# Putting a chunk's column sums behind its last query product, and normalising the second chunk behind all of the first

## The chip, the cores and the metric

The kernel runs on one core of one Trainium2 chip. The metric is the device time in microseconds (us) of one execution. A core has five engines with a queue of instructions each, and an engine works through its own queue in order: TensorE (PE, matrix products; PEld is its weight load), VectorE (DVE), ScalarE (ACT), GpSimd (POOL) and SyncE (SP, which only starts DMAs here). Engines wait for each other by semaphores. Matrix products write to PSUM banks, and a bank can be written again only when its result has been read out ("evacuated").

## What is computed

One layer of a hybrid decoder: a normalised input is projected into the operands of three mixers (stick-breaking attention, a Mamba-2 scan, latent attention), whose outputs are joined and projected back, and a gated feed-forward block and a last norm follow. The change lies in the very first part, the norm and the first projections:

```python
def rmsnorm(x, g):
    xf = x.astype(F32)
    y = xf * lax.rsqrt(jnp.mean(xf * xf, axis=-1, keepdims=True) + EPS)
    return (y * g.astype(F32)).astype(x.dtype)
...
        hn = rmsnorm(h, mix_norm_g[i])
        proj = hn @ w_in[i].astype(dt)
        sb_q, sb_k, sb_v, ssm_z, ssm_xbc, ssm_dt, c_q, c_kv, k_r = jnp.split(proj, split_at, axis=-1)
```

All tensors are float32; there are 1024 tokens and 16 meta tokens, 1024 features and one layer.

## The kernel before, in words

Tensors stand feature-major: 8 tiles of 128 features by 1040 tokens. Each float32 operand of a product is split into a rounded part ("hi") and the rest ("lo"), and each product is done as three: hi by hi, lo by hi, hi by lo (`dense_fm`, lines 147 to 149: 8 feature tiles by 3, so 24 products into one PSUM bank; there are two such banks, `d_ps`, used in turn).

The 1040 tokens are worked on in three chunks of 272, 384 and 384 columns (chunks 0, 1, 2). To start the products early, chunks 0 and 1 aren't normalised first. Their operands are the input times the gain alone (`first_operands`, lines 239 and 240: ACT writes the hi part `hnh`, DVE the lo part `hnl`), and the result is multiplied by the reciprocal root mean square of each token when it is evacuated. That factor comes from `chunk_rstd`: ACT squares the 8 tiles, DVE adds them up in `acc` (line 255), PE sums `acc` over the features by three small products (`ssum`, line 158), DVE scales the sums (`rc`, lines 167 and 169), POOL takes the power -0.5 (line 170), PE spreads the result over all partitions (`rrow`, line 176) and ACT copies it into `row` (line 262).

Then for chunk i the loop at line 648 issues the key product (weights `wk`), the query product (`wq`) and the value products of its token blocks (`sb_values`, lines 575 to 577, weights `wv`, banks `v_ps`). The key's evacuation `k_evac` multiplies by `row` (DVE, line 596: `scaled`) and splits into `K` and `KS` (ACT lines 603 and 604, DVE lines 605 and 606); the query's does the same into `Q` (lines 612 and 613). The lo parts of the first weights are made by POOL, one subtraction each (line 231), the hi parts by ACT (line 230).

Chunk 2, and all later products, use normalised operands: `normalise` multiplies by gain and `row` (DVE, line 270), rounds (ACT, line 271) and subtracts (DVE, line 272), 8 tiles each. `normalise(2)` is put behind the query evacuation of chunk 0 (`issue_after(scored)`), and `normalise(0)` and `normalise(1)` both behind `normalise(2)`. The first product that reads normalised chunks 0 and 1 is that of the step sizes (`step_sizes`, line 432, weights `whi`, `wlo`), which follows the value products of chunk 2 and a few score products (`sc_ps`, line 685).

A scheduler sets the order of each engine's queue at build time, by priorities that the code hands out (`high_priority`) and by `issue_after`, which keeps what is written under it behind a given instruction; PE, DVE and ACT each get one fixed order. So a change at the start can also turn neighbours round much later in the program.

Of the kernel before, what the change touches and what calls it, by code (L numbers as in the profile page):

```python
# [21 lines left out]
KT = D // 128  # L22
SEQ = 1024
META = 16
# [15 lines left out]
CH_ALL = [(0, 272), (272, 384), (656, 384)]  # L40
CH_REAL = [(0, 512), (512, 512)]
CH_SHORT = [(0, 384), (384, 384), (768, 256)]
BLOCKS = [(0, META)] + [(META + 128 * b, 128) for b in range(NQ)]
# [16 lines left out]
def tile_hybrid_block(ctx: ExitStack, tc: tile.TileContext, a: dict):  # L60
# [3 lines left out]
    PE, DVE, ACT, SP = (getattr(mybir.EngineType, e) for e in ("PE", "DVE", "Activation", "SP"))  # L64

    def last_on(engine):
        return next(i for i in reversed(nc.cur_bb.bb.instructions) if i.engine == engine)

    def f32(ap):
        return ap.bitcast(F32)  # L70
# [68 lines left out]
    def dense_fm(dpool, w, nkt, m, mov, chunks, evac):  # L139
        hi, lo = w  # L140
        for c0, n in chunks:
            ps = dpool.tile([128, 512], F32, tag="d", name="d_ps")
            for kt in range(nkt):
                mh, ml = mov(kt, c0, n)
                wh = hi[:, kt * m : (kt + 1) * m]
                wl = lo[:, kt * m : (kt + 1) * m]
                pe.matmul(ps[:m, :n], wh, mh, start=(kt == 0), stop=False)  # L147
                pe.matmul(ps[:m, :n], wl, mh, start=False, stop=False)  # L148
                pe.matmul(ps[:m, :n], wh, ml, start=False, stop=(kt == nkt - 1))  # L149
            with tc.high_priority(offset=1000):  # L150
                evac(ps, c0, n)

    def token_rstd(cols, ps, squares, blocks, width, bufs=1):


        for e, (t0, w) in enumerate(blocks):
            for i, sq in enumerate(squares):
                pe.matmul(
                    ps[:w, e : e + 1], sq[:, t0 : t0 + w], ones[:, 0:1], start=(i == 0), stop=(i == len(squares) - 1)
                )  # L160
        nb = len(blocks)
        r = cols.tile([128, nb], F32, tag=f"rc{nb}", bufs=bufs, name="rc")
        e0 = 0
        if blocks[0][1] < 128:
            w = blocks[0][1]
            dve.memset(r[:, 0:1], 1.0)
            dve.tensor_scalar(r[:w, 0:1], ps[:w, 0:1], 1.0 / width, EPS, ALU.mult, ALU.add)
            e0 = 1
        dve.tensor_scalar(r[:, e0:nb], ps[:, e0:nb], 1.0 / width, EPS, ALU.mult, ALU.add)
        pool.tensor_tensor(r, r, mhalf[:, :nb], op=ALU.pow)  # L170
        return r
# [8 lines left out]
    dpool = ctx.enter_context(tc.tile_pool(name="dpsum", bufs=2, space=PSUM))  # L180
# [15 lines left out]
    def fill_tile(tag, name):  # L196
        return fl.tile([128, 388 if tag == "craw" else 384], F32, tag=tag, name=name)
# [36 lines left out]
    def first_operands(i):  # L234

        c = slice(CH_ALL[i][0], sum(CH_ALL[i]))
        for k in range(KT):
            g = gmix[:, k : k + 1]
            act.activation(HH[k][:, c], xT[:, k, c], AF.Identity, scale=g)
            dve.scalar_tensor_tensor(HL[k][:, c], xT[:, k, c], g, f32(HH[k][:, c]), ALU.mult, ALU.subtract)  # L240

    def chunk_rstd(i):
        c0, n = CH_ALL[i]
        blocks = [(t0 - c0, w) for t0, w in BLOCKS[3 * i : 3 * i + 3]]
        if i == 2:
            squares = [raws[k // 2][:, 512 * (k % 2) :][:, :n] for k in range(KT)]
        else:
            acc = fill_tile("cacc", "acc")[:, :n]
            squares = [acc] + [sqs[k % 2][:, 512 * (k // 2 % 2) :][:, :n] for k in range(1, KT)]
        acc = squares[0]  # L250
        for k in range(KT):
            x = xT[:, k, c0 : c0 + n]
            act.activation(squares[k], x, AF.Square)
            if k > 0:
                dve.tensor_tensor(acc, acc, squares[k], op=ALU.add)
        ssum = ps0.tile([128, 4], F32, tag="ssum", name="ssum")
        with tc.high_priority(offset=200):
            r = token_rstd(p0, ssum, [acc], blocks, D, bufs=3)
            rrow = ps0.tile([128, 512], F32, tag="rrow", bufs=1, name="rrow")
            spread(rrow, r, blocks, 0)  # L260
            row = p0.tile([128, 384], F32, tag="row", bufs=3, name="row")
            act.copy(row[:, :n], rrow[:, :n])
        return r, row

    def normalise(i, row):
        c0, n = CH_ALL[i]
        c = slice(c0, c0 + n)
        for k in range(KT):
            hn = xT[:, k, c]
            dve.scalar_tensor_tensor(hn, hn, gmix[:, k : k + 1], row[:, :n], ALU.mult, ALU.mult)  # L270
            act.copy(HH[k][:, c], hn)
            dve.tensor_tensor(HL[k][:, c], hn, f32(HH[k][:, c]), op=ALU.subtract)
# [346 lines left out]
    proj, k_evac, q_evac = sb_project(0)  # L619
# [5 lines left out]
    w_k = first_weight(raws[0], a["w_sbk"][0], *first_pair("wk"), (dve, pool), dve)  # L625
    load_x(0, (2, 4, 6))
    first_operands(0)
    w_q = first_weight(raws[1], a["w_sbq"][0], *first_pair("wq"), (pool,))
    stats = [chunk_rstd(0)]
    w_v = []  # L630
    for u in range(2):
        both = value_tile("wv")
# [14 lines left out]
    sp.dma_start(acol, a["a_log"].partition_broadcast(128))  # L647
    for i, (q0, qn) in enumerate(((0, 256), (256, 384), (640, 384))):
        c0, n = CH_ALL[i]
        if i == 0:  # L650
            first_operands(1)
            stats += [chunk_rstd(1), chunk_rstd(2)]
        if i < 2:
            r, row = stats[i]
            dense_fm(dpool, w_k, KT, 128, hn_mov, [(c0, n)], lambda ps, t0, m: k_evac(ps, t0, m, row[:, :m]))
            t1 = META + q0 - c0
            dense_fm(dpool, w_q, KT, 128, hn_real, [(q0, qn)], lambda ps, t0, m: q_evac(ps, t0, m, row[:, t1 : t1 + m]))
            scored = last_on(DVE)
            sb_values(0, w_v, range(3 * i, 3 * i + 3), r, ps0)
            if i == 0:  # L660
                with tc.issue_after(scored):
                    normalise(2, stats[2][1])
                normal = last_on(DVE)
            with tc.issue_after(normal):
                normalise(i, row)
        else:
            dense_fm(dpool, w_k, KT, 128, hn_mov, [(c0, n)], k_evac)
            dense_fm(dpool, w_q, KT, 128, hn_real, [(q0, qn)], q_evac)
            sb_values(0, w_v, range(3 * i, 3 * i + 3), None, ps0)
    p0_st.close()  # L670

    with ctx_sb as st:
# [40 lines left out]
        for p in range(4):  # L713
            sb_attend(p, proj, values)
            if p < 3:
                if p == 1:
                    sb_values(1, [load_w(a["w_sbv"][1, u]) for u in range(2)], range(9))
                proj, k_evac, q_evac = sb_project(p + 1)
# [20 lines left out]
    with ExitStack() as st:  # L739
# [159 lines left out]
        for b, (t0, w) in enumerate(BLOCKS):  # L899
            ps = bank()  # L900
# [493 lines left out]
    acc = [squares(0, fs, eng) for fs, eng in (((0, 1, 2), pool), ((3, 4, 5), dve), ((6,), dve), ((7,), dve))]  # L1394
# [3 lines left out]
    with tc.high_priority(offset=400):  # L1398
        r = row_sums(acc)
        summed = last_on(PE)  # L1400
        row = row_spread(*r)
# [15 lines left out]
    acc = [squares(1, (0, 1, 4), pool)]  # L1417
# [14 lines left out]
    with tc.high_priority(offset=400):  # L1432
        r = row_sums(acc)
        summed = last_on(PE)
        row = row_spread(*r)
# [238 lines left out]
    r1, row = last_part(512, 256, between=r0)  # L1674
    last_norm(0, 512, row, (3, 6), 2)
    r2, row = last_part(768, 256, True, r1)
# [90 lines left out]
```

## Time and profile before

| | us |
|---|---|
| median of 3 runs | 1768.85 |
| the runs | 1763.76, 1768.85, 1770.01 |
| the profiled execution | 1767.26 |
| its span on the core | 1765.5 |

| engine | busy us | share of the span |
|---|---|---|
| PE | 1704.5 | 97% |
| DVE | 1143.8 | 65% |
| ACT | 846.2 | 48% |
| POOL | 721.3 | 41% |

The 1.8 us between the profiled execution and its span lie around the program and don't change with it. PE is busy nearly all of the time, so its idle stretches, and the stretches in which it runs at the lower of its two clock levels, are what an edit of the order can win or lose. In a timeline row the first number is the start, the second the length in us, and the bracket at the end is the time that the engine idled before and what ended that. Rows of one kind are merged (x8).

### The profile page before, as it was taken

Reading aid. Unit: us, or ns where it says so; the run is one execution under the profiler, and the core shown is the slowest. Engines: PE = TensorE matmul, PEld = TensorE weight load, DVE = VectorE, ACT = ScalarE, POOL = GpSimd, SP = SyncE. Lnnn points to the kernel's source line nnn. Section 1 sums busy time; section 2 is a strip of 40 time slices with the busy share of each in tenths; the row PEclk is TensorE's granted clock in tenths of the full one; section 3 lists DMA queues with packets and bytes.
Section 4 is the critical chain, followed back from the end, with each engine's and each line's share of the span. In section 5 each row is a group of like instructions: output and inputs, shape, how many; then the busy total and the mean of one; then the engine's idle time right before and its main releaser. Section 6 shows DMA issues by size and latency. Waiting matters only on the chain. (4 is left out here: it accounts for less than half of the span.)

```text
span 1765.5 us, 26574 instructions
## 1 busy us (share of the span) xinstructions
PE 1704.5 (97%) x9801; PEld 1496.5 (85%) x9801; DVE 1143.8 (65%) x1742; ACT 846.2 (48%) x1797; POOL 721.3 (41%) x498
## 2 busy tenths in 40 slices
PE   8979999999998999999999999999999999999998
PEld 7869989999987778998888878778888888878887
DVE  7678767678544673555575646986566766678644
ACT  6545565656466646676454425432322232244332
POOL 3234335334467566563331346544455545200012
PEclk9999999999999999999999999999999999999998
DMA  4222232222443546347331443122323223999602
GB/s 161 73 64 64 65 91 73 59 66 74 127 130 114 187 158 175 112 125 235 121 90 31 121 147 111 60 84 96 114 96 108 96 90 106 310 388 374 245 1 96
DMA packets 145638, 222.35 MB, mean 126 GB/s; under 512 B 24722, under 2 KB 84148, under 8 KB 145508
## 3 DMA queue, kind: packets, MB, share of 16 engines
q1 hardware_dynamic: 126112, 205.09, 36.0%
q10 hardware_dynamic: 19396, 15.56, 2.8%
q8 instruction: 77, 1.26, 0.3%
q14 instruction: 53, 0.43, 0.1%
HBM read 157.56 MB, written 63.04 MB: 125 GB/s over the span
## 5 line engine op out<-in xcount | busy, mean ns | idle before, releaser
L147 PE MATMUL d_ps<-hnh,whi 128*128 128x384 f32 (+6 forms) x744 | 249.8, 336 | 12.1 <-DVE KS L606 9.9
L149 PE MATMUL d_ps<-hnl,whi 128*128 128x384 f32 (+6 forms) x744 | 246.6, 332 | 0.0
L148 PE MATMUL d_ps<-hnh,wlo 128*128 128x384 f32 (+6 forms) x744 | 246.1, 331 | 0.0
L136 POOL TENSOR_TENSOR wlo<-wraw,whi 128x1024 fp32r<-128x1024 f32 (+1 forms) x57 | 141.1, 2475 | 227.0 <-ACT whi L134 226.2
L147 PEld LDWEIGHTS d_ps<-hnh,whi 128*128 128x128 f32 (+1 forms) x744 | 140.5, 189 | 18.0 <-issue 11.5
L149 PEld LDWEIGHTS d_ps<-hnl,whi 128*128 128x128 f32 (+1 forms) x744 | 140.8, 189 | 2.9 <-issue 0.2
L148 PEld LDWEIGHTS d_ps<-hnh,wlo 128*128 128x128 f32 (+1 forms) x744 | 140.6, 189 | 3.0 <-issue 0.5
L1274 PE MATMUL b_ps<-T,wl 128*128 128x512 f32 x352 | 138.8, 394 | 1.3 <-POOL wl L1105 1.3
L1275 PE MATMUL b_ps<-T,wh 128*128 128x512 f32 x352 | 138.2, 394 | 1.3 <-DVE T L1105 1.3
L1273 PE MATMUL b_ps<-T,wh 128*128 128x512 f32 x352 | 139.1, 396 | 0.0
L311 DVE TENSOR_TENSOR pl<-ptg,ph 128x512 fp32r<-128x512 f32 (+1 forms) x160 | 99.3, 627 | 43.0 <-ACT ph L310 41.5
L1104 ACT CAST op<-raw 128x1024 fp32r<-128x1024 f32 x69 | 71.3, 1050 | 108.1 <-PE d_ps L1559 64.4
L1105 DVE TENSOR_TENSOR op<-raw,op 128x1024 fp32r<-128x1024 f32 x69 | 84.8, 1239 | 41.6 <-ACT op L1104 41.5
L693 DVE TENSOR_TENSOR_SCAN cm<-cm,zcol 128x144 f32<-128x144 f32 (+3 forms) x64 | 101.8, 1594 | 13.3 <-ACT cm L691 12.9
L310 ACT CAST ph<-ptg 128x512 fp32r<-128x512 f32 (+1 forms) x160 | 85.2, 543 | 51.8 <-PE ptg L327 29.7
L1105 POOL TENSOR_TENSOR wlo<-raw,whi 128x1024 fp32r<-128x1024 f32 x18 | 45.4, 2523 | 109.5 <-ACT whi L1104 109.5
L1105 POOL TENSOR_TENSOR wl<-raw,wh 128x512 fp32r<-128x512 f32 x46 | 74.4, 1625 | 29.4 <-ACT wh L1104 29.4
L1104 ACT CAST wh<-raw 128x512 fp32r<-128x512 f32 x88 | 53.1, 616 | 66.4 <-PE b_ps L1275 66.3
L1111 POOL TENSOR_TENSOR tt<-tt 128x512 f32<-128x512 f32 (+1 forms) x8 | 8.1, 1012 | 186.7 <-ACT tt L1629 186.5
L134 ACT CAST whi<-wraw 128x1024 fp32r<-128x1024 f32 (+1 forms) x57 | 59.0, 1035 | 48.6 <-DMA wraw<-in_w_o_dram 17.2
L1274 PEld LDWEIGHTS b_ps<-T,wl 128*128 128x128 f32 x352 | 66.5, 189 | 16.8 <-POOL wl L1105 1.6
L1275 PEld LDWEIGHTS b_ps<-T,wh 128*128 128x128 f32 x352 | 66.3, 188 | 16.7 <-DVE T L1105 1.6
(442 smaller groups left out, 5171.9 us busy)
## 6 DMA issues: line engine op xcount, KB each, us to landing
raw<-in_w_down_dram SPq DMA_DIRECT2D x99, 256.0 KB, 5.3
s_hops<-gs SPq DMA_DIRECT2D x63, 256.0 KB, 2.0
raw<-s_hops SPq DMA_DIRECT2D x63, 256.0 KB, 5.3
raw<-in_w_gate_dram SPq DMA_DIRECT2D x22, 512.0 KB, 3.6
raw<-in_w_up_dram SPq DMA_DIRECT2D x22, 512.0 KB, 4.0
wraw<-in_w_o_dram SPq DMA_DIRECT2D x16, 512.0 KB, 4.2
wraw<-in_w_xbc_dram SPq DMA_DIRECT2D x12, 512.0 KB, 3.6
s_xs<-csig SPq DMA_DIRECT2D x24, 192.0 KB, 2.4
```

The costliest lines, as they stand in the source:

```text
L136: pool.tensor_tensor(lo[:, :cols], raw[:, :cols], f32(hi[:, :cols]), op=ALU.subtract)
L147: pe.matmul(ps[:m, :n], wh, mh, start=(kt == 0), stop=False)
L148: pe.matmul(ps[:m, :n], wl, mh, start=False, stop=False)
L149: pe.matmul(ps[:m, :n], wh, ml, start=False, stop=(kt == nkt - 1))
L310: act.copy(ph[:, :n], pt[:, :n])
L311: dve.tensor_tensor(pl[:, :n], pt[:, :n], f32(ph[:, :n]), op=ALU.subtract)
L693: dve.tensor_tensor_scan(rev, rev, zcol.to_broadcast([128, n_all]), 1.0, ALU.mult, ALU.add)
L1104: act.copy(hi, value)
L1105: eng.tensor_tensor(lo, value, f32(hi), op=ALU.subtract)
L1273: pe.matmul(banks[j], hi[:, ks], UH[u][k], start=start and k == 0, stop=False, skip_group_check=skip)
L1274: pe.matmul(banks[j], lo[:, ks], UH[u][k], start=False, stop=False, skip_group_check=skip)
L1275: pe.matmul(banks[j], hi[:, ks], UL[u][k], start=False, stop=stop and k == 3, skip_group_check=skip)
```

## The change

`chunk_rstd` is split in two. `chunk_squares` holds the squares and their sum, `chunk_rstd` the small products and what follows them. The key and query products of chunks 0 and 1 are issued with an evacuation that only remembers its arguments (`held`); for chunk 0 the small products are kept behind the last query product (`issue_after(last_on(PE))`), the operands and sums of chunks 1 and 2 follow, and then the evacuations of both products are issued, at high priority. `normal` is moved on after each `normalise`, so that chunk 1 is normalised behind all of chunk 0.

```diff
-    def chunk_rstd(i):
+    def chunk_squares(i):
         c0, n = CH_ALL[i]
...
             if k > 0:
                 dve.tensor_tensor(acc, acc, squares[k], op=ALU.add)
+        return acc
+
+    def chunk_rstd(i, acc):
+        n = CH_ALL[i][1]
+        blocks = [(t0 - CH_ALL[i][0], w) for t0, w in BLOCKS[3 * i : 3 * i + 3]]
         ssum = ps0.tile([128, 4], F32, tag="ssum", name="ssum")
...
-    stats = [chunk_rstd(0)]
+    first = chunk_squares(0)
...
-        if i == 0:
-            first_operands(1)
-            stats += [chunk_rstd(1), chunk_rstd(2)]
         if i < 2:
+            t1 = META + q0 - c0
+            held = []
+            dense_fm(dpool, w_k, KT, 128, hn_mov, [(c0, n)], lambda *at: held.append(at))
+            dense_fm(dpool, w_q, KT, 128, hn_real, [(q0, qn)], lambda *at: held.append(at))
+            if i == 0:
+                with tc.issue_after(last_on(PE)):
+                    stats = [chunk_rstd(0, first)]
+                first_operands(1)
+                stats += [chunk_rstd(e, chunk_squares(e)) for e in (1, 2)]
             r, row = stats[i]
-            dense_fm(dpool, w_k, KT, 128, hn_mov, [(c0, n)], lambda ps, t0, m: k_evac(ps, t0, m, row[:, :m]))
-            t1 = META + q0 - c0
-            dense_fm(dpool, w_q, KT, 128, hn_real, [(q0, qn)], lambda ps, t0, m: q_evac(ps, t0, m, row[:, t1 : t1 + m]))
+            with tc.high_priority(offset=1000):
+                k_evac(*held[0], row[:, :n])
+                q_evac(*held[1], row[:, t1 : t1 + qn])
...
             with tc.issue_after(normal):
                 normalise(i, row)
+            normal = last_on(DVE)
```

On PE, at the end of chunk 0's key product, the order before was (`ssum` are the small products of the column sums, `wq` the query product, `wv` the value products; lines 575 to 577 of before are 579 to 581 of the changed file):

```order
L149 MATMUL d_ps<-hnl_146,wk 128x272
L147 MATMUL d_ps<-hnh_131,wq 128x256
L158 MATMUL ssum<-ones,acc 16x1
L158 MATMUL ssum<-ones,acc 128x1 x2
L575 MATMUL v_ps<-wv,hnh_131 16x256
L576 MATMUL v_ps<-wv,hnl_139 16x256
```

In the changed kernel the same place and, 22 query products further on, the place behind the last of them read:

```order
L149 MATMUL d_ps<-hnl_146,wk 128x272
L147 MATMUL d_ps<-hnh_131,wq 128x256
L579 MATMUL v_ps<-wv,hnh_131 16x256
L580 MATMUL v_ps<-wv,hnl_139 16x256
...
L149 MATMUL d_ps<-hnl_146,wq 128x256
L158 MATMUL ssum<-ones,acc 16x1
L158 MATMUL ssum<-ones,acc 128x1 x2
L579 MATMUL v_ps<-wv,hnh_131 128x256
L580 MATMUL v_ps<-wv,hnl_139 128x256
L581 MATMUL v_ps<-wv,hnh_131 16x256
```

The small products moved behind all 24 query products and six value products. The two value products that now follow them already belong to chunk 1.

On DVE, between the evacuations of chunk 1 and the end of the normalising, the order before was (384 wide are chunks 1 and 2, 272 wide is chunk 0; the first row of line 270 is chunk 2; `K<-d_ps` and `KS<-d_ps` empty the key bank of chunk 2):

```order
L606 TENSOR_TENSOR KS<-scaled,K 64x384
L596 TENSOR_TENSOR scaled<-d_ps,row 128x384
L613 TENSOR_TENSOR Q<-scaled,Q 64x384 x2
L270 SCALAR_TENSOR_TENSOR xT<-xT,gmix,row 128x384 x8
...
L270 SCALAR_TENSOR_TENSOR xT<-xT,gmix,row 128x272 x8
L270 SCALAR_TENSOR_TENSOR xT<-xT,gmix,row 128x384 x7
...
L270 SCALAR_TENSOR_TENSOR xT<-xT,gmix,row 128x384
L605 TENSOR_TENSOR K<-d_ps,K 64x384
L606 TENSOR_TENSOR KS<-d_ps,K 64x384
L613 TENSOR_TENSOR Q<-d_ps,Q 64x384
```

In the changed kernel the same stretch reads (lines 270, 272, 596, 605, 606 and 613 are now 274, 276, 600, 609, 610 and 617):

```order
L610 TENSOR_TENSOR KS<-scaled,K 64x384
L274 SCALAR_TENSOR_TENSOR xT<-xT,gmix,row 128x384 x8
L600 TENSOR_TENSOR scaled<-d_ps,row 128x384
...
L274 SCALAR_TENSOR_TENSOR xT<-xT,gmix,row 128x272 x7
L617 TENSOR_TENSOR Q<-scaled,Q 64x384 x2
L274 SCALAR_TENSOR_TENSOR xT<-xT,gmix,row 128x272
...
L274 SCALAR_TENSOR_TENSOR xT<-xT,gmix,row 128x384 x8
L617 TENSOR_TENSOR Q<-d_ps,Q 64x384
L609 TENSOR_TENSOR K<-d_ps,K 64x384
L610 TENSOR_TENSOR KS<-d_ps,K 64x384
```

Chunk 2's normalising moved ahead of chunk 1's query evacuation, and the second half of chunk 2's key evacuation moved ahead of the eight subtractions (line 276, 384 wide) of chunk 1.

Far behind the edit, among the gates of the Mamba part and the latent attention, POOL's order before was (`gy<-gy,gs` is the gate's product, on which the evacuation of a `d_ps` bank waits; `mlo<-st,mhi` are lo parts of the latent attention's operands):

```order
L544 TENSOR_TENSOR gy<-gy,gs 128x384
L967 TENSOR_TENSOR mlo<-st,mhi 96x1040
L517 TENSOR_TENSOR grow<-grow,sq 128x384
L967 TENSOR_TENSOR mlo<-st,mhi 96x1024
L136 TENSOR_TENSOR wlo<-wraw,whi 128x1024
```

In the changed kernel the same place reads (lines 544, 967 and 517 are now 548, 978 and 521):

```order
L978 TENSOR_TENSOR mlo<-st,mhi 96x1040
L978 TENSOR_TENSOR mlo<-st,mhi 96x1024
L548 TENSOR_TENSOR gy<-gy,gs 128x384
L136 TENSOR_TENSOR wlo<-wraw,whi 128x1024
L521 TENSOR_TENSOR grow<-grow,sq 128x384
```

Both subtractions moved ahead of the gate's product; the same is so at one other place of that stage.

## Rows read from the trace of the kernel before

**Rows 1.** The list of what PE waited for in the first 130 us: engine, tile and line, what it waited for, then total us, times and the longest.

```profile
PE d_ps L147 <- DVE KS L606: 8.4, 3, 3.4
PE d_ps L147 <- DVE wk L228: 5.6, 1, 5.6
PE ssum L158 <- DVE acc L255: 2.3, 1, 2.3
```

**Rows 2.** The timeline of PE, from the first query product to the first value products of chunk 1.

```profile
12.73 0.38 PE L147 MATMUL d_ps<-hnh,wq 128*128 128x256 f32 x1
15.46 1.14 PE L158 MATMUL ssum<-ones,acc 128*16 128x1 f32 x6 [2.35 <-DVE acc L255]
16.46 0.37 PE L575 MATMUL v_ps<-wv,hnh 128*16 128x256 f32 x1
...
17.70 0.41 PE L148 MATMUL d_ps<-hnh,wq 128*128 128x256 f32 x1
...
22.18 0.41 PE L148 MATMUL d_ps<-hnh,wq 128*128 128x256 f32 x1
...
26.34 0.28 PE L575 MATMUL v_ps<-wv,hnh 128*128 128x256 f32 x1
...
27.77 0.28 PE L575 MATMUL v_ps<-wv,hnh 128*128 128x256 f32 x1
...
31.51 0.72 PE L158 MATMUL ssum<-ones,acc 128*128 128x1 f32 x6
32.10 0.37 PE L577 MATMUL v_ps<-wv,hnh 128*128 128x256 f32 x1
```

**Rows 3.** The table by stretches: from:to and length in us, then busy us (and instructions) of PE, PEld, DVE, ACT and POOL, then PE's granted clock as a share of its upper level (1.00 is 2.4 GHz, 0.50 is 1.2 GHz), the DMA share and GB/s.

```profile
13.00:14.00 1.00, 0.11 (x1) 0.00 (x0) 1.00 (x1) 1.00 (x2) 1.00 (x1) 1.00 1.07 399
...
15.00:16.00 1.00, 0.54 (x4) 0.52 (x5) 0.40 (x1) 1.00 (x4) 1.00 (x2) 0.81 1.07 393
...
21.00:22.00 1.00, 1.00 (x7) 1.00 (x7) 1.00 (x2) 0.11 (x1) 0.31 (x1) 0.50 0.22 83
...
23.00:24.00 1.00, 1.00 (x11) 0.79 (x10) 1.00 (x3) 1.00 (x3) 0.00 (x0) 1.00 0.00 0
...
69.00:72.00 3.00, 0.14 (x2) 0.00 (x0) 1.58 (x4) 2.89 (x7) 2.40 (x2) 1.00 0.13 45
...
103.00:107.00 4.00, 0.60 (x4) 0.32 (x3) 3.89 (x8) 1.57 (x4) 0.00 (x0) 1.00 0.19 58
...
108.00:109.00 1.00, 1.00 (x3) 0.73 (x3) 1.00 (x1) 0.61 (x2) 1.00 (x2) 0.50 0.00 1
```

**Rows 4.** The timelines of ACT (first row), POOL (five rows) and DVE (two rows), the weights' hi and lo parts and what lies beside them.

```profile
12.58 1.99 ACT L230 CAST wv<-raw 128x1024 fp32r<-128x1024 f32 x2
...
12.75 2.35 POOL L231 TENSOR_TENSOR wq<-raw,wq 128x1024 fp32r<-128x1024 f32 x1 [4.32 <-ACT wq L230]
15.06 2.57 POOL L231 TENSOR_TENSOR wv<-raw,wv 128x1024 fp32r<-128x1024 f32 x1
...
18.75 2.57 POOL L231 TENSOR_TENSOR wv<-raw,wv 128x1024 fp32r<-128x1024 f32 x1
32.85 1.10 POOL L170 TENSOR_TENSOR rc<-rc,mhalf 128x3 f32<-128x3 f32 x1 [11.54 <-DVE rc L169]
...
59.65 5.27 POOL L136 TENSOR_TENSOR wlo<-wraw,whi 128x768 fp32r<-128x768 f32 x1 [19.30 <-ACT whi L134]
...
12.31 3.09 DVE L255 TENSOR_TENSOR acc<-acc,sqs 128x272 f32<-128x272 f32 x2
...
18.97 3.29 DVE L240 SCALAR_TENSOR_TENSOR hnl<-xT,gmix,hnh 128x384 fp32r<-128x384 f32 x2
```

**Rows 5.** The timeline of DVE, from chunk 1's key evacuation to the release of chunk 2's key bank.

```profile
41.63 0.56 DVE L606 TENSOR_TENSOR KS<-scaled,K 64x384 fp32r<-64x384 f32 x1
...
45.31 4.33 DVE L270 SCALAR_TENSOR_TENSOR xT<-xT,gmix,row 128x384 f32<-128x384 f32 x8
49.55 3.83 DVE L272 TENSOR_TENSOR hnl<-xT,hnh 128x384 fp32r<-128x384 f32 x8
53.30 7.10 DVE L270 SCALAR_TENSOR_TENSOR xT<-xT,gmix,row 128x272 f32<-128x272 f32 x15
60.31 2.90 DVE L272 TENSOR_TENSOR hnl<-xT,hnh 128x272 fp32r<-128x272 f32 x8
63.23 0.55 DVE L605 TENSOR_TENSOR K<-d_ps,K 64x384 fp32r<-64x384 f32 x1
...
71.33 0.56 DVE L606 TENSOR_TENSOR KS<-d_ps,K 64x384 fp32r<-64x384 f32 x1
```

**Rows 6.** The timeline of PE: the start of chunk 2's products, the first score product behind its value products, and the first product of the step sizes.

```profile
50.94 0.33 PE L147 MATMUL d_ps<-hnh,wk 128*128 128x384 f32 x1
...
67.85 0.23 PE L685 MATMUL sc_ps<-K,Q 128*128 128x144 f32 x1
...
72.03 0.34 PE L147 MATMUL d_ps<-hnh,whi 128*96 128x272 f32 x1 [2.89 <-DVE KS L606]
```

**Rows 7.** The timeline of POOL at the place of the gates that the change turns round.

```profile
746.29 1.01 POOL L544 TENSOR_TENSOR gy<-gy,gs 128x384 f32<-128x384 f32 x1 [3.60 <-ACT gs L543]
749.26 2.44 POOL L967 TENSOR_TENSOR mlo<-st,mhi 96x1040 fp32r<-96x1040 f32 x1 [1.96 <-ACT mhi L966]
...
752.62 2.40 POOL L967 TENSOR_TENSOR mlo<-st,mhi 96x1024 fp32r<-96x1024 f32 x1
```

More of the change, by code (lines that the diff above doesn't have):

```diff
@@ L240, in first_operands @@
             dve.scalar_tensor_tensor(HL[k][:, c], xT[:, k, c], g, f32(HH[k][:, c]), ALU.mult, ALU.subtract)
-    def chunk_rstd(i):
+    def chunk_squares(i):
         c0, n = CH_ALL[i]
-        blocks = [(t0 - c0, w) for t0, w in BLOCKS[3 * i : 3 * i + 3]]
         if i == 2:
```

## The prediction

> **What bounds the kernel now.** I read the page's busy shares first: PE is busy 97% of the span, so time can come only from PE's idle stretches and from stretches at its lower clock level. The list of PE's waits in the first 130 us [rows 1] is to show the reader three kinds: 5.6 us at the very start for the first weight, which the change leaves alone; 2.35 us in which the column sums of chunk 0 wait for DVE's last addition; and three waits, 8.4 us together, for a key bank that DVE has not emptied. The change touches the second kind directly and the first of the three bank waits by order.
>
> PE's timeline [rows 2] shows what the 2.35 us hold up. The sums stand behind one query product that ended at 13.11 (12.73 + 0.38); they start at 15.46, and the value products and the other 23 query products, which don't need the sums, queue behind them. Then the table by stretches [rows 3]: PE's granted clock is 1.00 (2.4 GHz) at 13 to 14 and falls to 0.50 (1.2 GHz) during 15 to 16, after the idle stretch; it is still 0.50 at 21 to 22 and 1.00 at 23 to 24. So the wait also cost some 7 us at the lower level.
>
> Why does DVE end so late? Its last two additions took 3.09 us instead of some 0.9 [rows 4]: the second one finished only as POOL's subtraction for `wq` ended at 15.10.
>
> Last, DVE's timeline and the place where PE waits on it [rows 5, 6]: chunk 2's key bank is released when the second `KS` ends at 71.89, because 7 of chunk 1's normalising products stood ahead of it; PE had run out of work at about 69 and waited 2.89 us.
>
> **The wait for the sums.** Removed: 2.35 us of idle time. What is late next? The value products need the hi part of `wv`: two casts take 1.99 us from 12.58, so the first is there at about 13.6, and PE waits 0.5 us. Six value products at the upper level take 6 x 0.119 = 0.7 us (0.119 from 12 steps between 26.34 and 27.77) and end at 14.3. The next query product needs `wq`'s lo part, ready at 15.10 [rows 4]: another 0.75 us. 2.35 - 1.25 = 1.1 us are won.
>
> **The clock.** In place of one gap of 2.35 us stand two short ones with products between them. Rows show a fall after 2.35 us of idle at 13 to 15.5 and after 3.40 us at 103 to 107, and none after 2.89 us at 69 to 72 [rows 3], so the fall isn't certain even with long gaps, and I take it that two gaps under 0.8 us don't bring it. Then 29 products (6 value, 23 query) run at 0.119 instead of 0.213 us (22.18 - 17.70 over 21 steps): 29 x 0.094 = 2.7 us. The six small sums took 1.00 us from start to next start at the lower level and 0.59 at the upper [rows 2]: 0.4 us. Together 3.1 us; 0 if the clock falls all the same.
>
> **What the later sums bring.** Query products then end at 15.10 + 23 x 0.119 = 17.8, the sums at 18.4. Two value products of chunk 1 follow at once, the second of which needs DVE's first lo part of chunk 1. DVE is free at 15.40 but blocked until POOL's first `wv` subtraction ends (17.63); then the lo part takes 0.54 and is there at 18.2, in time. For the reciprocal roots DVE has 4 such operations and 2 additions ahead of `rc`: 4 x 0.54 + 2 x 0.48 = 3.1 us (a row of 8 each at that width [rows 5]), and POOL's second `wv` subtraction, 2.35 us, holds it up once: 17.63 + 3.1 + 2.35 = 23.1. POOL's power takes 1.10 [rows 4]: 24.2. PE reaches `rrow` 39 value products after the sums, 18.4 + 4.6 = 23.0, and now waits 1.2 us for it. Before, that row was ready long ahead. The sums of chunk 1 come next: DVE has 4 lo parts and 6 additions more, 23.1 + 5.1 = 28.2; PE is there at 24.2 + 0.6 + 24 x 0.119 = 27.7 and waits 0.5 us. Behind chunk 1's last addition DVE has four additions of chunk 2 (4 x 0.48) and then reads chunk 0's key bank (some 0.4): empty at about 30.5; PE, with 19 value products more, asks for it at 31. New waits: 1.7 us. If PE is at its lower clock it comes later and these waits vanish, so clock and waits offset each other in part.
>
> Front, summed: 1.1 + 3.1 - 1.7 = 2.5 us earlier at the end of chunk 2's value products: 65.3 instead of 67.85.
>
> **The bank wait at 72.** DVE's queue is now: 8 normalising products of chunk 2 directly behind chunk 1's key evacuation, without the query evacuation that stood ahead. The key evacuation ended at 42.2 and ends 2.5 us earlier, 39.7; chunk 2's `row` comes from a spread behind 14 of the 24 query products of chunk 1 and is copied at about 40.6, which sets the start (before: 45.31). From there to the release of chunk 2's key bank DVE works [rows 5]: 4.33 + 0.56 + 3.83, then 3.3 for the 8 narrow products (7.10 less 7 x 0.54), 1.1 (query, chunk 1), 2.90, 1.1 (first half of the key), 4.33 (chunk 1), 0.56, 1.1 = 23.1 us, so 63.7. PE asks at 65.3 (the score products now stand behind, so they cover nothing). The 2.89 us go. What could be late next is the same release: POOL's subtraction for the step sizes took 5.27 us beside DVE [rows 4], of which 1.8 is its own by size (2.35 x 768/1024); if all of that falls on DVE, the release is at 65.5 and PE waits 0.2. I take 0.4 off for this and what I can't see: 2.5 us.
>
> Chunk 1 behind all of chunk 0 costs nothing by itself: the step sizes read chunk 0 first, and chunk 1's last lo part, some 4.5 us behind the release, is there before PE has done chunk 0's 24 products and the scores.
>
> **The rest.** The number of operations is the same, so nothing is added in busy time. The stores and reloads of the values follow PE's earlier end. Later, the order changes among the gates and the latent attention; PE waits little there in the trace. I take 0, with bounds below.
>
> **Sum.** 2.5 + 2.5 = 5.0 us off the profiled execution: 1767.3 - 5.0 = 1762.3. It stands 1.6 under the median of the runs, so against that median the forecast is **1764**. About 0.5% (8.8 us) is what a measurement of this kernel can tell from no change, so this is a gain inside "the same".
>
> **A rule that speaks against it.** Rows 4 show DVE's addition ending just behind POOL's subtraction, and a lo part of chunk 1 stretched to 3.29 us for two beside the next. The Trainium skill, "SBUF — State Buffer", section "SBUF: two separate sides", says that VectorE with two SBUF inputs and GpSimd share a port pair as an exclusive lock held for a whole instruction, and that the loser blocks. The trace agrees in both places. It does not say who gets the lock when both wait. If POOL ran both `wv` subtractions in a row, chunk 1's first lo part would come at 15.40 + 2 x 2.35 + 0.54 = 20.6 instead of 18.2, with PE standing at it from 18.5: the second rival's mechanism. DVE's addition ran between POOL's two at 15.06 to 15.40, which is why it isn't my forecast.
>
> **Rivals.**
> *The wait only changes its name* (1766, chance 0.22). The two short gaps bring the clock down all the same, or PE stands at chunk 1's first lo part for some 2 us. For it: the sums now need DVE and POOL in their most crowded stretch. Then the front wins 1.1 us at most and only the bank wait goes: about 3 us, 1768.85 - 3 = 1766.
> *More follows* (1758, chance 0.12). The two other bank waits, 8.4 - 2.89 = 5.5 us, shrink too: DVE's key evacuations of the next pair queue behind scans and step-size arithmetic, and one scan now stands behind an evacuation. For it: these waits lower the clock too (0.50 at 108). Against: what stands ahead of them on DVE is the same work, started by PE's own products, so it moves along with PE. 5.0 + 5.5 = 10.5 us.
> *The gates pay* (1773.5, chance 0.12). At two places of the gate stage POOL now does both subtractions of the latent attention, 2.44 and 2.40 us, ahead of the gate's product [rows 7], which started at 746.29 while the first subtraction had its data only at 749.26. The bank of the gate is held that much longer; it decides if PE has less than 4.8 us of other work before it asks for that bank. Then 2 x 4.8 = 9.6 us are lost against 5.0 won: 4.6 slower than before. Against: PE's own order there was rearranged with it, and PE waits hardly at all in that stage.
> The forecast holds 0.54.
>
> **Range and chances.** Half of the third case lies above 1771 and half of the second below 1757; with the runs' own spread of 6 us some 0.2 lie outside 1757 to 1771. Faster by over 0.5% means under 1760.0: most of "more follows" and a tail of the forecast, 0.14. Slower by over 0.5% means over 1777.7: a third of "the gates pay", 0.04. The rest, 0.82, is no change that can be told.
>
> **What would show it.** In the profile after: no wait of the sums for DVE at 13 to 15.5, two gaps under 1 us there, and granted clock 1.00 from 13 through 24; if it is 0.50 at 16 to 20, the clock step is wrong. A new wait of PE at `rrow` of 1 to 1.5 us near 23, for POOL's power. No wait at the first step-size product, which starts near 65; a wait there of more than 0.7 us would make the DVE walk wrong. Two bank waits for the next pair remain, about 5 us earlier. In the gate stage, the list of waits shows new rows of some us if the third rival is true.

## The result, and the profile after

| | before | after |
|---|---|---|
| median of 18 runs each, us | 1768.14 | 1757.84 |
| the runs, us | 1763.02 to 1772.89 | 1754.74 to 1762.98 |
| the profiled execution, us | 1767.26 | 1762.44 |
| its span, us | 1765.5 | 1760.7 |
| PE busy, us | 1704.5 | 1706.4 |

The ratio of the times is 0.9949, with a 95% interval of 0.994 to 0.9958: 1768.14 x 0.0051 = 9.0 us faster, just over the 0.5% that can be told from no change. Between the two profiled executions only 4.8 us lie (1765.5 - 1760.7): the profile after shows one of the slower runs of its kernel. Both the cause of the gain and the missing 4 us had to be found.

The list of PE's waits in the first 130 us after the change (total us, times, longest), which answers to [rows 1]:

```profile
PE sc_ps L696 <- ACT cm L702: 3.6, 1, 3.6
PE d_ps L147 <- DVE KS L610: 3.1, 2, 2.0
PE ptg L329 <- ACT acs L478: 2.4, 1, 2.4
...
PE rrow L176 <- POOL rc L170: 0.7, 1, 0.7
...
PE d_ps L148 <- POOL wq L231: 0.4, 1, 0.4
PE v_ps L579 <- ACT wv L230: 0.3, 1, 0.3
```

The wait of the sums (2.3) is gone, and of three bank waits (8.4) two are left (3.1). A wait of a score product for ACT, 3.6 us, is new. The 2.4 us of `ptg` are not: before, the same wait stands at 130.60, just behind this stretch. PE's timeline, which answers to [rows 2] and [rows 6]:

```profile
14.08 0.40 PE L579 MATMUL v_ps<-wv,hnh 128*16 128x256 f32 x1 [0.26 <-ACT wv L230]
...
15.59 0.39 PE L148 MATMUL d_ps<-hnh,wq 128*128 128x256 f32 x1 [0.45 <-POOL wq L231]
...
18.50 0.74 PE L158 MATMUL ssum<-ones,acc 128*16 128x1 f32 x6
...
24.66 1.03 PE L176 MATMUL rrow<-identr,rc 16*128 16x16 f32 x6 [0.71 <-POOL rc L170]
...
28.48 0.80 PE L158 MATMUL ssum<-ones,acc 128*128 128x1 f32 x6
...
65.44 0.29 PE L147 MATMUL d_ps<-hnh,whi 128*96 128x272 f32 x1
```

The last row, the first step-size product, has no bracket: PE didn't wait for chunk 2's key bank. It starts 6.59 us earlier than the 72.03 of before; 1.29 us of that is nine score products (67.85 to 69.14 before), which now stand behind it. So 5.3 us were won up to here. The table by stretches (columns as in [rows 3]; the share of 2.4 GHz stands behind POOL's) has 1.00 where it had 0.81 and 0.50:

```profile
15.00:16.00 1.00, 0.55 (x5) 0.41 (x4) 1.00 (x2) 1.00 (x3) 1.00 (x2) 1.00 1.07 392
21.00:22.00 1.00, 1.00 (x10) 1.00 (x10) 1.00 (x3) 0.28 (x1) 0.00 (x0) 1.00 0.30 102
```

In the second row PE does 10 products where it did 7. DVE and POOL, which answer to [rows 4] and, in the last two rows, to [rows 5]:

```profile
15.76 2.77 DVE L240 SCALAR_TENSOR_TENSOR hnl<-xT,gmix,hnh 128x384 fp32r<-128x384 f32 x1
...
15.49 2.62 POOL L231 TENSOR_TENSOR wv<-raw,wv 128x1024 fp32r<-128x1024 f32 x1
...
18.05 2.75 POOL L231 TENSOR_TENSOR wv<-raw,wv 128x1024 fp32r<-128x1024 f32 x1
...
58.34 4.31 DVE L274 SCALAR_TENSOR_TENSOR xT<-xT,gmix,row 128x384 f32<-128x384 f32 x8
...
63.84 0.56 DVE L610 TENSOR_TENSOR KS<-d_ps,K 64x384 fp32r<-64x384 f32 x1
```

Chunk 1's first lo part was held until POOL's first `wv` subtraction ended at 18.11 and was ready at 18.53. The key bank is released at 64.40 (63.84 + 0.56) instead of 71.89.

How far the lead went shows when the same instruction is looked up in both traces. Three places serve: the first step-size product (72.03 before), a product of the next pair (149.04 before), and the first product behind a wait in the gate stage (671.96 before). All kernels that were run, with the difference in us to the first profile of before (minus is earlier); the last column is the ratio of the times (e10 is a single execution; at 149 a blank stands where the products around that place have another order):

| kernel | step sizes | at 149 | at 672 | span | ratio [95%] |
|---|---|---|---|---|---|
| after | -6.6 | -6.6 | -7.1 | -4.8 | 0.9949 [0.994, 0.9958] |
| e1, after again | -6.7 | -7.0 | -7.6 | -11.2 | 0.9951 [0.9937, 0.9965] |
| e2, sums only | -1.4 | +1.8 | +0.6 | +1.4 | 0.9992 [0.9982, 1.0003] |
| e3, chain only | +3.8 | +3.9 | +2.8 | +3.3 | 1.0010 [0.9999, 1.0021] |
| e4, filler | -0.5 | +0.9 | -0.8 | +4.7 | 1.0012 [1.0002, 1.0023] |
| e5, early release | -3.8 | -8.3 | -3.6 | +0.7 | 0.9992 [0.998, 1.0004] |
| e6, filler and early release | -5.5 | -7.2 | -9.0 | -7.9 | 0.9951 [0.9939, 0.9963] |
| e7, sums and early release | -6.8 | -0.5 | -1.5 | -1.6 | 0.9990 [0.9979, 1.0001] |
| e8, arithmetic late | -6.2 | | +7.9 | +12.5 | 1.0036 [1.0022, 1.005] |
| e9, arithmetic behind rows | -6.4 | | -5.2 | -3.4 | 0.9971 [0.9959, 0.9982] |
| e10, before again | -0.9 | -1.9 | -2.3 | +0.4 | |

(In after, e1 and e5 to e9 the nine score products, 1.3 us, stand behind the first step-size product instead of ahead. e9 and e10 ran on another chip than e1 to e8.)

### The profile page after: what moved, and what is told of

It reads as the page before. It is cut to its first block, busy times and chain, and to the rows that moved or that the text cites. A ratio compares the mean times of both kernels' runs of the same rounds, so it can differ in the third digit from the quotient of the medians.

```text
span 1760.7 us, 26573 instructions
## 1 busy us (share of the span) xinstructions
PE 1706.4 (97%) x9801; PEld 1500.3 (85%) x9801; DVE 1140.2 (65%) x1742; ACT 846.2 (48%) x1797; POOL 720.0 (41%) x498
## 5 line engine op out<-in xcount | busy, mean ns | idle before, releaser
L147 PEld LDWEIGHTS d_ps<-hnh,whi 128*128 128x128 f32 (+1 forms) x744 | 141.0, 190 | 12.5 <-issue 6.1
L1012 ACT ACTIVATE pr<-sc_ps,sm 128x256 f32<-128x256 f32 (+4 forms) x112 | 59.8, 540 | 46.8 <-DVE sm L1009 24.8
L502 DVE SCALAR_TENSOR_TENSOR cacc<-d_ps,cw,cacc 128x384 f32<-128x384 f32 (+3 forms) x108 | 61.7, 571 | 29.5 <-ACT cacc L495 27.4
```

## The experiments

**e1: the changed kernel again.** No edit.

> The changed kernel once more, unchanged, for a second profile. The first profile gained only 4.8 us on the span (1765.5 to 1760.7) while the medians gained 10.3. Theory 'the front is firm, the gate stage scatters': the second profile agrees with the first to 0.5 us up to 660 us (value products of chunk 2 end at 65.4, no wait at the first step-size product, clock 1.00 from 13 to 24), and what differs between two executions arises between 670 and 1100 us, in granted clock and waits; ratio 0.993 to 0.997. Rival 'the front scatters': the two profiles differ by over 2 us already at 150 us.

At the step sizes, at 149 and at 672 the two profiles agree within 0.5 us. At the end they lie 6.4 us apart (1760.7 and 1754.3). The table by stretches of 10 us, first of the changed kernel's first profile, then of its second:

```profile
1070.00:1080.00 10.00, 9.79 (x47) 8.54 (x47) 3.66 (x4) 3.85 (x7) 7.05 (x5) 0.66 0.45 161
1090.00:1100.00 10.00, 9.97 (x51) 8.20 (x50) 5.66 (x8) 7.16 (x12) 6.04 (x5) 0.83 0.07 26
1120.00:1130.00 10.00, 7.40 (x24) 5.38 (x23) 10.00 (x14) 3.19 (x8) 8.16 (x6) 0.83 0.26 84
```

```profile
1070.00:1080.00 10.00, 8.42 (x46) 6.99 (x46) 4.89 (x8) 3.45 (x5) 5.58 (x5) 1.00 0.33 93
1090.00:1100.00 10.00, 10.00 (x55) 8.51 (x55) 7.80 (x13) 4.49 (x8) 2.33 (x2) 1.00 0.00 0
1120.00:1130.00 10.00, 10.00 (x43) 7.93 (x43) 10.00 (x11) 3.43 (x6) 7.06 (x6) 1.00 0.38 106
```

Much the same work meets a granted clock of 0.66 to 0.83 in one execution and 1.00 in the other. Between the first product of line 1385 (1032.88 and 1030.82) and one of line 1286 (1123.68 and 1117.71) the two part from 2.1 to 6.0 us: most of the missing us lie there. Up to 672 us this kernel is firm. Its median here (1761.07 of 6 runs) is higher than in the first series, the ratio the same.

**e2: the sums alone**, without the chaining.

```diff
             with tc.issue_after(normal):
                 normalise(i, row)
-            normal = last_on(DVE)
```

> The held sums and the late evacuations alone; chunk 1 is normalised behind chunk 2 as before. Theory 'two parts, each with its own gain': the front is as in the changed kernel (no wait at 13 to 15.5 over 1 us, clock 1.00 to 24, value products of chunk 2 end near 65.4), but five or six of chunk 1's normalising products (0.54 us each) stand ahead of the key bank's release again, so PE waits 2 to 3.5 us at the first step-size product; gain 2.5 us at that place instead of 5.3, ratio 0.996 to 0.999. Rival 'the sums do it all': no wait there over 0.7 us and the same ratio as the changed kernel, 0.995.

Ratio 0.9992: the two-parts theory, and less than it expected. The front is as in the changed kernel (last value product at 65.21), but PE then stands 4.06 us. PE's row, a stretch behind it (columns as in [rows 3]), and DVE's rows ahead of the release:

```profile
70.67 0.51 PE L147 MATMUL d_ps<-hnh,whi 128*96 128x272 f32 x1 [4.06 <-DVE KS L610]
```

```profile
72.00:73.00 1.00, 1.00 (x6) 1.00 (x5) 0.18 (x1) 0.74 (x1) 0.56 (x2) 0.50 0.46 3
```

```profile
53.35 4.74 DVE L274 SCALAR_TENSOR_TENSOR xT<-xT,gmix,row 128x272 f32<-128x272 f32 x6
...
67.77 1.14 DVE L274 SCALAR_TENSOR_TENSOR xT<-xT,gmix,row 128x384 f32<-128x384 f32 x2
...
69.97 0.56 DVE L610 TENSOR_TENSOR KS<-d_ps,K 64x384 fp32r<-64x384 f32 x1
```

Chunk 1's normalising products stand ahead of the release again (five in the first row, two in the second, one between), and six of its lo parts with them. The release comes at 70.53, 1.36 us earlier than in the kernel before (71.89), and so does the step-size product: the lead of 2.5 us that PE had is worth only what DVE brings forward. And the longer wait costs more than itself: the clock is at 0.50 behind it, the 24 step-size products of chunk 0 take 5.07 us (70.67 to 75.74) instead of 3.05 before (72.03 to 75.08), and with that the lead is gone.

**e3: the chaining alone**, on the kernel before.

```diff
             with tc.issue_after(normal):
                 normalise(i, row)
+            normal = last_on(DVE)
```

> The chaining alone: chunk 1 is normalised behind all of chunk 0, the sums stay where they were. Theory 'two parts': idle 2.35 us at 13 to 15.5 and the fall of the clock to 0.50 remain, value products end at 67.85. DVE's order there is 8 narrow products, 8 narrow lo parts, 8 wide products, then the key's first half, 8 wide lo parts and the second half: the release of the key bank comes at 71.89 + one lo part, 0.5 us, and five more score products (0.8 us) stand ahead of the step sizes on PE, so the wait there is 2.0 to 3.0 us: no gain by itself, ratio 0.998 to 1.001. Rival 'the chain takes the bank wait away on its own': wait under 0.7 us, gain 2.5 us or more by 75 us, ratio 0.996 to 0.998.

Ratio 1.0010: no gain, as expected, but by another wait than I had worked out. PE's rows and the stretch at 21:

```profile
21.52 0.41 PE L148 MATMUL d_ps<-hnh,wq 128*128 128x256 f32 x1
...
74.60 0.58 PE L686 MATMUL sc_ps<-K,Q 128*128 128x256 f32 x1 [5.18 <-ACT cm L692]
...
75.86 0.43 PE L147 MATMUL d_ps<-hnh,whi 128*96 128x272 f32 x1
```

```profile
21.00:22.00 1.00, 1.00 (x7) 1.00 (x6) 1.00 (x1) 0.71 (x2) 0.93 (x1) 1.00 0.38 138
```

Fourteen score products stand ahead of the step sizes; the fourth score bank waits 5.18 us for ACT, and the release, behind all eight lo parts of chunk 1, comes only at 74.05. The second fence is a warning: the column of the granted clock says 1.00, but 7 products in the stretch, spaced 0.213 us as before, show the lower level. The durations decide.

**e4: the clock alone.** 20 products that nobody reads fill PE's wait for the sums.

```diff
+            if i == 0:
+                for _ in range(20):
+                    pe.matmul(rrow[:, :256], w_q[0][:, :128], HH[0][:, :256], start=True, stop=True)
             r = token_rstd(p0, ssum, [acc], blocks, D, bufs=3)
```

> The kernel before, with 20 products of 128x256 whose results nobody reads put on PE into the 2.35 us that it waits for the column sums (20 x 0.119 = 2.4 us). Nothing else is taken away: the sums still start at about 15.5. Theory 'the idle stretch brings the clock down': with PE busy the clock stays at 1.00 from 13 to 24 and the value and query products behind it run at 0.119 us instead of 0.213, so chunk 2's value products end 2.5 to 3.2 us earlier, near 65, and the kernel gains about 3 us, ratio 0.997 to 0.999. Rival 'the clock falls at that time anyway': granted clock 0.50 at 16 to 22, value products end at 67.9 or later, ratio 1.000.

```profile
13.12 2.61 PE L261 MATMUL rrow<-hnh,wq 128*128 128x256 f32 x20
15.67 0.74 PE L158 MATMUL ssum<-ones,acc 128*16 128x1 f32 x6
...
28.48 0.80 PE L158 MATMUL ssum<-ones,acc 128*128 128x1 f32 x6 [0.96 <-DVE acc L255]
...
71.56 0.51 PE L147 MATMUL d_ps<-hnh,whi 128*96 128x272 f32 x1 [3.91 <-DVE KS L609]
```

Ratio 1.0012. The first half of the theory holds: with PE busy the clock stays up. From the start of the sums to the first value product of chunk 1 PE takes 4.24 us (15.67 to 19.91) with one product more, against 7.09 before (15.46 to 22.55): 2.85 + 0.12 = 3.0 us for the clock, where the prediction had 3.1. The second half falls: 0.96 us go back to chunk 1's sums, and the rest of the lead into the bank wait (3.91 instead of 2.89), because DVE's release stays at 71.4. Here too the products behind the longer wait run at the lower level at first: the 24 take 4.35 us (71.56 to 75.91) instead of 3.05. PE's time at the front is worth nothing while that release is late.

**e5: the release early, nothing else.** On the kernel before, chunk 1 is normalised behind chunk 2's key evacuation.

```diff
-            with tc.issue_after(normal):
-                normalise(i, row)
+            if i == 0:
+                with tc.issue_after(normal):
+                    normalise(i, row)
...
             dense_fm(dpool, w_k, KT, 128, hn_mov, [(c0, n)], k_evac)
+            with tc.issue_after(last_on(DVE)):
+                normalise(1, stats[1][1])
```

> The kernel before, with the sums where they were, and chunk 1's normalising put behind the key evacuation of chunk 2 (the release of its bank) instead of behind chunk 2's normalising. In the first three experiments neither the sums (0.9992) nor the chain (1.0010) nor the clock (1.0012) gained anything alone, and in each PE stood 2.9 to 5 us near 70 for what DVE or ACT had late. Theory 'the release of chunk 2's key bank is the gate, and the front only pays once it is early': the release comes near 62 to 63 instead of 71.9, the 2.89 us wait is gone, the first step-size product follows the last value product (67.9) at once; gain 2.9 us or more at that place, and some of it stays: ratio 0.996 to 0.9985. Rival 'only both together gain': another wait of 2 us or more takes its place before 80 us (chunk 1's lo parts, a score product), ratio 0.999 or more.

The release comes at 63.53, the wait is gone, and at 149 the kernel leads by 8.3 us, more than the changed kernel. But the ratio is 0.9992. At 672 the lead is 3.6 us; 4.8 went between 540 and there, where this kernel's order differs from that of before and after. Two of PE's rows there:

```profile
563.50 0.38 PE L794 MATMUL R<-A,sel 80*128 80x128 bf16 x4 [1.60 <-ACT L L806]
...
565.30 0.59 PE L794 MATMUL R<-A,sel 80*128 80x128 bf16 x4 [1.42 <-ACT L L806]
```

The next product, at 565.88, takes 0.79 us: PE is at the lower level again. The other 4.3 us go behind 672, where e10 loses 2.7 us without any edit. So the theory holds at its place and neither expectation covers the end: half of what the early edit wins goes in the scan stage, with the order that the scheduler then laid there; that this order is the cause is not shown by a run of its own.

**e6: filler and early release.** Both edits.

> The same early release, with the 20 unread products in the wait for the sums, so that the clock stays up. Theory 'the front pays once the release is early': value products end at 66.2 to 66.4 as with the filler alone (1.5 us earlier than before), the first step-size product follows at once, so 4.4 us gained at that place instead of the filler's 0.5; ratio 0.995 to 0.998, and 0.0005 to 0.0015 below the early release alone. Rival 'the clock is worth nothing': the same ratio as the early release alone.

```profile
66.56 0.29 PE L147 MATMUL d_ps<-hnh,whi 128*96 128x272 f32 x1
```

The first step-size product starts at 66.56 without a wait, 0.12 behind the last value product, and the lead is kept: ratio 0.9951, the same as the changed kernel, by another way. The difference to e5 (0.0041) can't be put down to the clock, since e5 lost its lead elsewhere.

**e7: sums and early release**, the chaining replaced by the release by name.

> The changed kernel's held sums, with the same early release by name in place of the chaining. Theory 'the chaining works only through the release': the first step-size product at 65.3 to 65.6 without a wait, as in the changed kernel, and the same ratio, 0.994 to 0.9965. Rival 'the chain has another use' (chunk 0 ready first): a ratio of 0.997 or more with the release as early.

```profile
65.26 0.29 PE L147 MATMUL d_ps<-hnh,whi 128*96 128x272 f32 x1
...
105.97 0.77 PE L147 MATMUL d_ps<-hnh,whi 128*128 128x512 f32 x1 [3.58 <-DVE KS L610]
...
116.11 0.74 PE L147 MATMUL d_ps<-hnh,whi 128*128 128x512 f32 x1 [2.54 <-DVE KS L610]
```

The first place is the changed kernel's (65.44), so there the chaining works through the release alone. But at 149 only 0.5 us are left, and the ratio is 0.9990, which is what the rival expected. Of the first score products only those of one row are issued within the step sizes (69.65), the others behind them (77.77 and later), and DVE's scans and step-size arithmetic reach the next pair's key evacuations later: bank waits of 3.58 and 2.54 us where the changed kernel has 1.15 and 1.99, each followed by products at the lower level (the second wait's first product takes 0.74). Whether chunk 0 ready first has a part in the changed kernel's gain, as the rival has it, is not shown.

**e8 and e9: can more be won?** In the changed kernel ACT's queue shows where the new 3.6 us come from:

```profile
83.21 0.65 ACT L702 ACTIVATE cm<-sc_ps 128x256 f32<-128x256 f32 x2
86.92 0.33 ACT L445 ACTIVATE d<-dx 128x144 f32<-128x144 f32 x1 [3.06 <-DVE dx L443]
...
87.92 1.28 ACT L446 ACT_TABLE_LOAD   x1
...
90.86 1.28 ACT L702 ACT_TABLE_LOAD   x1
92.16 0.38 ACT L702 ACTIVATE cm<-sc_ps 128x256 f32<-128x256 f32 x1
```

The sigmoid that frees the score bank stands behind the step sizes' Abs, which waits 3.06 us for DVE, and behind two table loads around Exp. Both experiments put this arithmetic (`step_chain`, cut out of `step_sizes`) later.

```diff
-                        with tc.issue_after(last_on(PE)):
-                            running_sums(decays)
+                        with tc.issue_after(last_on(PE)), tc.issue_after(last_on(ACT)):
+                            running_sums(step_chain(decays))
```

This is e9; in e8 the call stands behind the projections of the next pair.

> The changed kernel, with the arithmetic of the step sizes (ACT's Abs and Exp, DVE's 14 operations behind them) and the running sums put behind the projections of the next pair. Theory 'what is left near 92 and 102 to 111 is this arithmetic among the score products and evacuations': the 3.6 to 3.9 us wait of a score product for ACT (a table load to and fro around Exp) and the two bank waits of 3.1 to 3.5 us together shrink to under 3 us, the clock stays at 1.00 through 90 to 115, 4 us more gained by 130; ratio 0.990 to 0.993. Rival 'the waits only change their name': other waits of the same sum between 90 and 140, ratio 0.994 to 0.996; it could be slower where the running sums now hold up a later stage.

> The changed kernel, with the arithmetic of the step sizes put only behind the first pair of score rows, not behind the whole projections as in the run before it (which gained 8 us by 115 and lost 20 behind it). Theory 'the waits near 92 and 102 to 111 come from this arithmetic standing ahead of ready sigmoids and evacuations': the score product's 3.6 to 3.9 us and the bank waits' 3.1 to 3.5 us shrink to under 3 us together, 3 to 5 us gained by 130 against the changed kernel, ratio 0.991 to 0.994. Rival 'it is given back by the running sums, which now come later': 2 us or more of new waits between 110 and 160, ratio 0.994 to 0.998.

e8 is slower than the kernel before (1.0036): the bank waits do go (0.4 us is left), but from 130 on the attention waits for DVE. e9 (0.9971) is better than before and worse than the changed kernel. Its first query product of the next pair starts at 97.96, 8.8 us ahead of before (106.75); then one bank wait takes most of that:

```profile
109.51 0.77 PE L147 MATMUL d_ps<-hnh,whi 128*128 128x512 f32 x1 [5.74 <-DVE KS L614]
```

In both the waits change place, much as the rivals had it; e8 came out slower than either ratio that it named. No version beat the changed kernel.

**e10: the kernel before again.** No edit.

> The kernel before once more, unchanged, for a second profile of it. Theory 'the front is firm, the late stages scatter with the clock': the first value products, the first step-size product (72.0) and the place at 670 us agree with the first profile to 0.7 us; 670 to 1150 us may differ by up to 6 us, with other stretches at the lower clock. Rival 'the front of this kernel scatters': over 2 us apart already at 150 us.

The sums wait as before (2.32 us), but the clock comes back earlier:

```profile
19.00:20.00 1.00, 1.00 (x7) 1.00 (x6) 1.00 (x3) 1.00 (x3) 1.00 (x2) 0.51 1.16 343
20.00:21.00 1.00, 1.00 (x10) 1.00 (x10) 1.00 (x1) 1.00 (x4) 1.00 (x1) 1.00 0.91 305
```

It is 1.00 from 20 on, in the first profile only from 23. This front does scatter, by 0.9 us at the step sizes and 1.9 at 149, which lies between the two expectations; and the late stages take 2.7 us back (from -2.3 at 672 to +0.4). The term for the clock was taken from an execution in which the clock stayed low long. Since e10 ran on another chip, the difference can be the chip's as well as the execution's.

## Why the prediction was right or wrong

**The time.** The forecast was 1764, the median is 1757.84, and 9.0 us were won by the ratio instead of 5.0. The range holds it by 0.8 us (it begins at 1757), and a time under 1760.0 had a chance of only 0.14. The direction and the mechanism at the front are right; the size is half of what came.

**The wait for the sums.** Two waits of 0.26 and 0.45 us stand where 0.5 and 0.75 were forecast. The sums start at 18.50 and the next product at 19.10, where 17.8 and 18.4 were forecast: chunk 0's key product ended later (first query product at 13.41 instead of 12.73).

**The clock.** The column of the granted clock is at 1.00 from 13 to 24, as forecast, but it is so ahead of that too, while the products up to 14.5 start 0.20 to 0.23 us apart, at the lower level; in the profile before they came to the upper one at 12.1. From 14.6 on they start 0.119 us apart, and the wait of 0.45 us doesn't bring a fall. e4 shows that the idle stretch had brought the clock down and prices it at 3.0 us (3.1 forecast); in e10 the same stretch takes 5.55 us (15.93 to 21.48) instead of 7.09, 1.5 us less.

**What the later sums bring.** `rc` was forecast for 23.1 and is there at 23.3; POOL's power ends at 24.6 (24.2), PE waits 0.71 us (1.2) for it, and not at all for chunk 1's sums (0.5). The last value product starts at 65.32; 65.3 was forecast for their end. Two misses cancel in this: the sums end 0.7 us late, and of 1.7 us of new waits only 0.7 came. The prediction had said that a later PE would meet shorter waits, and priced neither. Chunk 1's first lo part was there at 18.53 (18.2), before PE asked for it, because DVE got its turn between POOL's two subtractions. By the Trainium skill, "SBUF — State Buffer", section "SBUF: two separate sides", VectorE with two SBUF inputs and GpSimd lock each other out for a whole instruction. The trace agrees here too: DVE's 2.77 us end 0.42 us behind POOL's first subtraction, and POOL's second takes 2.75 us.

**The bank wait at 72.** Release at 64.40 (63.7), no wait. Both front terms together, 5.0 forecast, measured 5.3. What the prediction did not see is that they aren't two gains to be added: e2, e3 and e4 take one each and win nothing. The reason stands in the prediction's own walk along DVE's queue (what sets the step sizes is the release), but I used it only to price the second edit; and behind the longer waits the clock falls (e2, e4).

**The step that failed: "The rest ... I take 0"**, and with it the argument that the next pair's bank waits move along with PE. Those two waits, before and after, and the new one:

```profile
106.75 0.48 PE L147 MATMUL d_ps<-hnh,whi 128*128 128x512 f32 x1 [3.40 <-DVE KS L606]
116.52 0.47 PE L147 MATMUL d_ps<-hnh,whi 128*128 128x512 f32 x1 [2.15 <-DVE KS L606]
```

```profile
92.59 0.45 PE L696 MATMUL sc_ps<-K,Q 128*128 128x400 f32 x1 [3.58 <-ACT cm L702]
101.95 0.47 PE L147 MATMUL d_ps<-hnh,whi 128*128 128x512 f32 x1 [1.15 <-DVE KS L610]
110.01 0.70 PE L147 MATMUL d_ps<-hnh,whi 128*128 128x512 f32 x1 [1.99 <-DVE KS L610]
```

The bank waits shrank from 5.55 us to 3.14, but the score wait takes more than that back: all named waits of PE between the step sizes and 120 sum to 6.5 us before and 6.7 after. Still the lead grew from 5.3 us to 6.6 at 149. The clock accounts for it: from the step sizes to the product at 149, products of 256 columns and more lose some 7.5 us at the lower level before, 6.1 after and 4.3 in e1 (an estimate: for each, the time to the next start beyond that of the same product at the upper level).

Behind 672 the lead first falls. At the first product of line 1374 (1036.44; line 1385 after) it is 3.6 us, and 5.6 in e1; e10, without any edit, falls by 2.6 us as well (from -2.3 to +0.3), so most of this loss need not be the new order's. From there to the end the profile after wins 1.2 us and e1 5.6, the latter with the clock. One wait there does go with the order:

```profile
1040.52 0.79 PE L1374 MATMUL d_ps<-raw,whi 128*128 128x512 f32 x1 [3.44 <-DVE hT L1083]
```

Both profiles of before have it, and e4, e5, e8 and e9 have one of 3.46 to 4.48 us at the same place; after, e1, e2, e3, e6 and e7 have none. In the table the kernels without it end between 0.3 us worse and 2.0 us better by the ratio than their lead at 672, those with it between 2.9 worse and 1.5 better. That points to some 2 us for the new order, which the prediction had at 0, but the scatter is as large: the ratio's 9.0 us less the lead at 672 would leave 1.4 to 1.9, counted from the second profile of before, whose front is 2.3 us faster, 3.7 to 4.2. No run changed the late order alone, so how much it is worth stays open.

**The rivals.** "More follows" (1758) has the time, but only a part of the mechanism: of the 5.5 us of bank waits 2.4 went, and the new score wait took them back. "The wait only changes its name" (the rival with PE standing at chunk 1's first lo part; the prediction once calls it the second) is refuted by the clock and the missing wait at chunk 1's lo part, though e2, e4 and e7 are cases of just that, one wait on. "The gates pay" is refuted: named waits of PE between 700 and 1000 sum to 5.9 us, against 5.2 before, none is for the gate's product, and the lead that goes from 672 to 1036 goes in e10 too.

## What to carry to other kernels

Before pricing an edit that lets an engine run ahead, find the next thing it must wait for and ask when that comes by its own engine's queue: the gain is the smaller of the two, and two edits that each win nothing can win 5 us together. A wait that grows can cost twice, as in e2, where the clock fell behind it. Behind an early edit in a scheduled program the order may be laid anew; e5 led by 8 us at 149 and by next to nothing at the end; so compare the same instruction at several places of both traces before giving an edit the credit for the end. And one profile of each kernel isn't enough where executions differ by 6 us.

## What was not expected of the hardware

The length of a wait doesn't tell whether the clock falls behind it. Products ran at the lower level after waits of 1.99 us (after, at 110: 0.70 us for the first), 2.54 (e7) and 4.06 (e2), but at the upper one after 3.00 in e6:

```profile
104.86 0.47 PE L147 MATMUL d_ps<-hnh,whi 128*128 128x512 f32 x1 [3.00 <-DVE KS L609]
```

In one and the same kernel, before, they ran at the upper level after the 2.89 us at 72 (0.34 for the first, [rows 6]) and in e10 at the lower one after 3.08 at the same place (0.47). The column of the granted clock can miss the lower level: e3 at 21, and the changed kernel up to 14.5. In the last stages much the same work met 0.66 in one execution and 1.00 in the next; most of the 6.4 us between the two profiles of the changed kernel arises there.
